# Low halves of the feed-forward projection's weight tiles from an accumulating transfer

## The chip, the cores and the metric

One core of a Trainium2 chip runs the whole program. The metric is the time of one execution on the device in microseconds, as the median of several runs; the profile is of one execution, taken by the hardware profiler.

## The reference

The program is one layer of a hybrid network on a sequence of 512 tokens of width 1024 in 32-bit floats: modulation of a normalised input, a mixer (an mLSTM beside an S5 state-space branch), a normalisation, a second modulation, and a gated feed-forward part. The change touches the first product of the feed-forward part alone:

```
def _conv_glu_ffn(h, w_ffn_up, w_ffn_conv, b_ffn_conv, w_ffn_down):
    val, gate = jnp.split(h @ w_ffn_up, 2, axis=-1)
    gate = jax.nn.gelu(_causal_dwconv(gate, w_ffn_conv, b_ffn_conv))
    return (gate * val) @ w_ffn_down
```

Here h is 512 x 1024 and w_ffn_up is 1024 x 5632, that is two halves of 2816 columns, or 2 x 22 tiles of 128 columns.

## The kernel before

The kernel gives TensorE its operands as float32r, and keeps the precision by splitting each operand into a high half (the operand written as float32r) and a low half (operand minus high half). A product is then the sum of three: high by high, high by low, low by high (`mm3`, L241 to L244). For a weight tile of 128 x 1024, `wsplit` (L224) does this in three steps: SP's queue loads the tile from HBM into a buffer w (`wload`, L215), ACT copies it into wh (L221), and DVE subtracts wh from w into wl (L210). There are 2 buffers of w, 3 of wh and 3 of wl; the next use of a buffer waits for the last reader of the one before.

The feed-forward projection has 44 such tiles, `h["wup"][u]`. Four of them (1, 0, 3, 2) are early: three use the three wh and wl buffers, one uses two others, and their products are taken over two halves of the tokens, each as soon as the normalised input of that half is there. The other 40 are split and multiplied in the loop over j (22 steps): first tile 2j + 1, the gate half, then tile 2j, the value half. A tile takes 8 times `mm3`, that is 24 matmuls of 512 columns, into a PSUM bank (`acc` for gate halves, 2 banks, and `hd` for value halves, 4 banks). The gate half goes through `gate_half`: POOL clears two columns of a buffer (L1183), ACT copies the bank behind them (L1184) and applies a scale and a bias (L1186), DVE adds the two other taps of the convolution (L202), and ACT and DVE compute the gelu (`gelu2`, L562 and L564). `val_half` multiplies by the value half (L207) and splits the result for the last product.

In the loop's steps 8 to 15, `ada2_step` also loads two 256 KB pieces of a modulation weight into buffers hh and adds them up on DVE.

The code is in program order, but the order of the instructions on each engine comes from a planner, which simulates the program with costs of its own and hands out each engine's instructions as they become ready there, those earlier in the program first; semaphores keep the dependencies. Each engine then runs its own queue in order, and transfers go out in the order of the queue that issues them. POOL issues no transfer in the kernel before; all go out on SP's queue.

Of the kernel before, what the change touches and what calls it, by code (L numbers as in the profile page):

```python
# [10 lines left out]
F32R = mybir.dt.float32r  # L11
I32 = mybir.dt.int32
AF = mybir.ActivationFunctionType
ALU = mybir.AluOpType
# [139 lines left out]
def build(tc, nc, h):  # L154
    with ExitStack() as ctx:
        _build(ctx, tc, nc, h)


def _build(ctx, tc, nc, h):
    V, A, T, GP = nc.vector, nc.scalar, nc.tensor, nc.gpsimd  # L160
# [4 lines left out]
    def tl(tag, shape, dt=F32, bufs=None, pool=None):  # L165
        uid[0] += 1
        return (pool or sb).tile(list(shape), dt, tag=tag, name=f"{tag}_{uid[0]}", bufs=bufs or BUFS[tag])
# [5 lines left out]
    def bank(tag):  # L173
        return tl(tag, [P, 512], pool=ps)
# [4 lines left out]
    def big(shape=(P, D), dt=F32, tag="hb"):  # L179
        return tl(tag, shape, dt)  # L180
# [10 lines left out]
    def dma(o, i):  # L191
        return nc.sync.dma_start(o, i)  # L192
# [16 lines left out]
    def sub(o, a, b):  # L209
        V.tensor_tensor(o, a, b, op=ALU.subtract)  # L210

    def f32(ap):
        return ap.bitcast(F32)

    def wload(ap, n=D, tag="w"):  # L215
        w = big(tag=tag)
        dma(w[:, :n], ap)
        return w

    def split_into(hi, lo, x):  # L220
        A.copy(hi, x)  # L221
        sub(lo, x, f32(hi))

    def wsplit(ap, n=D, tags=("wh", "wl"), w=None):  # L224
        w = wload(ap, n) if w is None else w
        wh, wl = (big(dt=F32R, tag=t) for t in tags)
        split_into(wh[:, :n], wl[:, :n], w[:, :n])
        return wh, wl

    def new_pair(tag):  # L230
# [494 lines left out]
    def kstep(j):  # L725
        wc = nxt[1]
        if j < KD - 1:
            nxt[:] = wa_load(j + 1), w0_load(j + 1)
        w0h, w0l = wsplit(None, NXM0 * P, w=wc)
        if j < KD - 1:  # L730
            pend = ada1_mm(j + 1, nxt[0])
        for m in range(NXM0):
            if j < KD - 1 and m == M1:
                ada1_cols(j + 1, *pend)
            if j < KD - 1 and m == M2:
                htr(j + 1)
            sl = slice(m * P, (m + 1) * P)
            mm3(acc0[m], w0h[:, sl], w0l[:, sl], hp[j][0], hp[j][1], j == 0, j == KD - 1)
# [13 lines left out]
    def ahead():  # L752
        while todo and len(ready) <= PF:
            ready.append(wsplit(todo.pop(0)))
        return ready.pop(0)
# [159 lines left out]
    def ada2_step(n=1):  # L915
        for _ in range(n):
            if not steps:
                return
            q, kc = steps.pop(0)
            if kc == 0:  # L920
                acc2[q] = [s5h(), s5h()]
            for i, a in enumerate(acc2[q]):
                wi = hh()
                dma(wi, h["wa2"][kc, :, q * D + i * 512:q * D + (i + 1) * 512])
                if kc == 0:
                    ts(a, wi, ca[:, 0:1])
                else:
                    stt(a, wi, ca[:, kc:kc + 1], a)
# [12 lines left out]
    def grow(i, factor):  # L941
        g = row(i)
        for n in range(2):
            o = bank("s5")
            for e, x in enumerate(pair_of(acc2[2 + i][n], "hh")):
                T.matmul(o, lhsT=onesr, rhs=x, start=e == 0, stop=e == 1)
            stt(g[n], o, 1.0, g[n], ALU.add, ALU.add)
            ts(g[n], g[n], factor)
        return g
# [45 lines left out]
    def scaled(src, g, st, tags=("wh", "wl")):  # L995
        w = wload(src)
        wh, wl = (big(dt=F32R, tag=t) for t in tags)
        for n in range(2):
            sl = slice(n * 512, (n + 1) * 512)
            x = w[:, sl] if st is None else tl(st, [P, 516])[:, :512]  # L1000
            tt(x, w[:, sl], g[n])
            split_into(wh[:, sl], wl[:, sl], x)
        return wh, wl
# [170 lines left out]
    def up_mm(o, w, c_):  # L1174
        for k in range(KD):
            sl = slice(k * P, (k + 1) * P)
            mm3(o[:, c_], w[0][:, sl], w[1][:, sl], h2[k][0][:, c_], h2[k][1][:, c_], k == 0, k == KD - 1)
# [3 lines left out]
    def gate_half(j, og):  # L1181
        gb_ = hh(514)
        GP.memset(gb_[:, 0:2], 0.0)  # L1183
        A.copy(gb_[:, 2:514], og)  # L1184
        a = hh()
        A.activation(a, og, AF.Identity, bias=col("fb", j), scale=col("fw", 44 + j))  # L1186
        for q in range(2):
            stt(a, gb_[:, q:q + 512], col("fw", 22 * q + j), a)
        gg = hh()
        gelu2(gg, a, hh)  # L1190
        return gg

    def val_half(j, gg, ov):
        tt(gg, ov, gg)
        gp_.append(pair_of(gg, "hp" if j < 8 else "hb" if j < 13 else "s5b" if j < 15 else "hx" if j < 18 else "gab"))

    early = [(u, wsplit(h["wup"][u], tags=("wh", "wl") if i < 3 else ("hb", "hb")), bank("hd"))
             for i, u in enumerate((1, 0, 3, 2)[:NS])]
    for hv in range(2):
# [10 lines left out]
    for j in range(NF):  # L1210
        if j == G2J:
            g2 = grow(1, 0.5)
        if j >= FJ:
            first.append(scaled(h["wfd"][len(first)], g2, None))
        ou = {}
        for u in (2 * j + 1, 2 * j):
            if u in pre:
                ou[u] = pre[u]
            else:
                w = wsplit(h["wup"][u])  # L1220
                ou[u] = bank("acc" if u % 2 else "hd")
                up_mm(ou[u], w, slice(0, 512))
            if u % 2:
                gg = gate_half(j, ou[u])
        val_half(j, gg, ou[2 * j])
        if 8 <= j < 16:
            ada2_step(1)
# [29 lines left out]
```

## Time and profile before

| what | value |
|---|---|
| median of 3 runs | 861.69 us (860.07 to 862.01) |
| span of the profiled execution | 862.0 us |
| TensorE busy | 828.5 us, 96% of the span |
| DVE busy | 607.1 us, 70% |
| ACT busy | 368.6 us, 43% |
| POOL busy | 98.0 us, 11% |
| read from HBM | 101.01 MB |

The span runs from the first to the last instruction of the profiled execution; no time around it is listed for that execution, so its own time is taken to be its span. The loop over the 40 tiles lies between about 506 and 730 us of it. In the rows, a line number such as L221 is that of the helper that issues the instruction, `wh<-w` names the tile that is written and those that are read, a bracket at the end of a row of the timeline is the idle time of the engine before that instruction and what ended it, and PE, DVE, ACT, POOL and SP are TensorE, VectorE, ScalarE, GpSimd and SyncE.

### The profile page before, as it was taken

How to read it: one execution, taken by the hardware profiler on the slowest of the kernel's cores; microseconds unless marked ns; L12 is line 12 of the kernel's file. 1: busy time of each engine (PE TensorE's matmuls, PEld its weight loads, DVE VectorE, ACT ScalarE, POOL GpSimd, SP SyncE). 2: the span in 40 equal slices, each digit the busy share in tenths (PEclk: the TensorE clock that was granted, in tenths of full speed). 3: DMA queues.
4: the chain of work that ended last, by engine and by line, in shares of the span. 5: the costliest groups of instructions: out<-in, count | busy, mean ns of one | idle time of the engine just before them, and what ended most of it. 6: DMA issues, size and time to landing. Idle time of an engine off the chain costs nothing.

```text
span 862.0 us, 11353 instructions
## 1 busy us (share of the span) xinstructions
PE 828.5 (96%) x4106; PEld 669.2 (78%) x4106; DVE 607.1 (70%) x1144; ACT 368.6 (43%) x589; POOL 98.0 (11%) x255
## 2 busy tenths in 40 slices
PE   3999999999999999999999999999999999999996
PEld 1777868778777778888887988888888878888785
DVE  5557978788689774578978767556777675878144
ACT  4454573564556442232334555444444444333000
POOL 2781211122022100000002200000000000000000
PEclk9999999999999999999999999999999999999998
DMA  9832132122222233568655023224444232445011
GB/s 336 288 132 86 53 101 62 45 85 62 79 60 87 86 123 122 196 203 294 210 191 177 2 74 102 94 98 147 146 147 137 86 120 74 171 163 169 11 49 49
DMA packets 45415, 105.94 MB, mean 123 GB/s; under 512 B 13360, under 2 KB 14256, under 8 KB 45360
## 3 DMA queue, kind: packets, MB, share of 16 engines
q1 hardware_dynamic: 45360, 105.23, 36.0%
q8 instruction: 32, 0.52, 0.2%
q14 instruction: 23, 0.19, 0.1%
HBM read 101.01 MB, written 2.10 MB: 120 GB/s over the span
## 4 chain that ended last, share of the span: by engine, by line
PE 76%; DVE 11%; ACT 4%; DMA 4%; issue 2%; SPq 2%; POOL 0%; DVEq 0%; ACTq 0%; POOLq 0%
PE acc L242 11%; PE acc L243 11%; PE acc L244 11%; PE hd L242 11%; PE hd L243 11%; PE hd L244 11%; DVE hh L202 2%; SPq L192 2%; DVE s5h L207 1%; PE s L242 1%; PE s L244 1%; PE s L243 1%; DVE wl L210 1%; PE s L612 1%; DMA w<-in_wmix 1%
## 5 line engine op out<-in xcount | busy, mean ns | idle before, releaser
L221 ACT CAST wh<-w 128x1024 fp32r<-128x1024 f32 (+2 forms) x103 | 103.2, 1003 | 144.0 <-PE acc L243 111.5
L210 DVE TENSOR_TENSOR wl<-w,wh 128x1024 fp32r<-128x1024 f32 (+2 forms) x103 | 120.5, 1172 | 60.8 <-ACT wh L221 60.1
L242 PE MATMUL acc<-hp,wh 128*128 128x512 f32 x256 | 103.4, 405 | 0.5 <-ACT hx L785 0.5
L244 PE MATMUL acc<-hp,wl 128*128 128x512 f32 x256 | 102.1, 399 | 0.0
L243 PE MATMUL acc<-hp,wh 128*128 128x512 f32 x256 | 102.1, 399 | 0.0
L242 PE MATMUL hd<-s5b,wh 128*128 128x512 f32 (+1 forms) x168 | 63.4, 380 | 0.7 <-ACT s5b L1169 0.5
L243 PE MATMUL hd<-s5b,wh 128*128 128x512 f32 (+1 forms) x168 | 63.6, 379 | 0.2 <-DVE s5b L210 0.2
L244 PE MATMUL hd<-s5b,wl 128*128 128x512 f32 (+1 forms) x168 | 63.3, 378 | 0.0
L242 PEld LDWEIGHTS acc<-hp,wh 128*128 128x128 f32 x256 | 48.2, 189 | 14.7 <-issue 3.7
L202 DVE SCALAR_TENSOR_TENSOR hh<-hh,hh 128x512 f32<-128x512 f32 x52 | 35.9, 691 | 31.2 <-ACT hh L564 14.7
L244 PEld LDWEIGHTS acc<-hp,wl 128*128 128x128 f32 x256 | 48.4, 189 | 11.2 <-issue 0.4
L243 PEld LDWEIGHTS acc<-hp,wh 128*128 128x128 f32 x256 | 48.4, 189 | 10.8 <-issue 0.4
L202 DVE SCALAR_TENSOR_TENSOR s5h<-hh,k,s5h 128x512 f32<-128x512 f32 x56 | 39.3, 746 | 4.7 <-DMA hh<-in_wa 4.6
L242 PEld LDWEIGHTS hd<-s5b,wh 128*128 128x128 f32 x168 | 31.3, 188 | 7.6 <-ACT s5b L1169 0.8
L243 PEld LDWEIGHTS hd<-s5b,wh 128*128 128x128 f32 x168 | 31.7, 189 | 7.0 <-DVE s5b L210 0.6
L244 PEld LDWEIGHTS hd<-s5b,wl 128*128 128x128 f32 x168 | 31.6, 188 | 6.4
L202 DVE SCALAR_TENSOR_TENSOR hh<-hh,k,hh 128x512 f32<-128x512 f32 x44 | 33.0, 751 | 4.5 <-ACT hh L1186 3.6
L1024 POOL TENSOR_SCALAR mov<-mov 128x1 f32<-128x1 f32 x6 | 3.7, 624 | 276.2 <-ACT s L1023 159.6
L244 PE MATMUL acc<-hx,wl 128*128 128x512 f32 x84 | 33.1, 394 | 0.0
L242 PE MATMUL acc<-hx,wh 128*128 128x512 f32 x84 | 33.1, 394 | 0.0
L243 PE MATMUL acc<-hx,wh 128*128 128x512 f32 x84 | 33.1, 394 | 0.0
L244 PE MATMUL acc<-s5b,wl 128*128 128x512 f32 x80 | 31.6, 395 | 0.5 <-DVE wl L210 0.5
(547 smaller groups left out, 2053.1 us busy)
## 6 DMA issues: line engine op xcount, KB each, us to landing
w<-in_wup SPq DMA_DIRECT2D x44, 512.0 KB, 3.2
hh<-in_wa SPq DMA_DIRECT2D x64, 256.0 KB, 4.2
w<-in_win SPq DMA_DIRECT2D x30, 512.0 KB, 3.2
w<-in_wfd SPq DMA_DIRECT2D x22, 512.0 KB, 3.3
hb<-in_wa SPq DMA_DIRECT2D x16, 512.0 KB, 7.4
w<-in_wglu SPq DMA_DIRECT2D x8, 512.0 KB, 3.3
w<-in_wdn SPq DMA_DIRECT2D x8, 512.0 KB, 3.3
w<-in_wmix SPq DMA_DIRECT2D x8, 512.0 KB, 4.2
```

The source lines that it names most:

```text
L192: return nc.sync.dma_start(o, i)
L202: V.scalar_tensor_tensor(o, i0, s, i1, op0=op0, op1=op1)
L207: V.tensor_tensor(o, a, b, op=op)
L210: V.tensor_tensor(o, a, b, op=ALU.subtract)
L221: A.copy(hi, x)
L242: T.matmul(o, lhsT=wh, rhs=xh, start=first, stop=False)
L243: T.matmul(o, lhsT=wh, rhs=xl, start=False, stop=False)
L244: T.matmul(o, lhsT=wl, rhs=xh, start=False, stop=last)
L612: T.matmul(o, lhsT=F[:, ri, pr, :], rhs=XB[:, ri, pr].rearrange("p g k -> p (g k)"), start=ri == 0, stop=False)
L1024: GP.tensor_scalar(v[:, 2:3], v[:, 0:1], v[:, 1:2], EPS * D, op0=ALU.add, op1=ALU.add)
```

## The change

The 40 tiles of the loop are split by a new function. The load of w and ACT's copy into wh stay. In place of DVE's subtraction, ACT writes the negated wh into wl, and then a transfer issued by POOL reads the same weight tile from HBM a second time and adds it to what stands in wl. The result is again the tile minus wh. DVE has no part in it. The four early tiles, and all other weights, are split as before by `wsplit`, which is unchanged.

```diff
--- before.py
+++ after.py
@@ -225,6 +225,14 @@
         w = wload(ap, n) if w is None else w
         wh, wl = (big(dt=F32R, tag=t) for t in tags)
         split_into(wh[:, :n], wl[:, :n], w[:, :n])
+        return wh, wl
+
+    def wsplit_dma(ap):
+        w = wload(ap)
+        wh, wl = (big(dt=F32R, tag=t) for t in ("wh", "wl"))
+        A.copy(wh, w)
+        A.activation(wl, f32(wh), AF.Copy, scale=-1.0)
+        GP.dma_start(wl, ap, accum_op=ALU.add)
         return wh, wl
 
     def new_pair(tag):
@@ -1217,7 +1225,7 @@
             if u in pre:
                 ou[u] = pre[u]
             else:
-                w = wsplit(h["wup"][u])
+                w = wsplit_dma(h["wup"][u])
                 ou[u] = bank("acc" if u % 2 else "hd")
                 up_mm(ou[u], w, slice(0, 512))
             if u % 2:
```

## Rows read from the trace of the kernel before

**Rows 1.** page: span, TensorE's busy time, transfers in 40 slices
```profile
span 862.0 us, 11353 instructions
...
PE 828.5 (96%) x4106; PEld 669.2 (78%) x4106; DVE 607.1 (70%) x1144; ACT 368.6 (43%) x589; POOL 98.0 (11%) x255
...
GB/s 336 288 132 86 53 101 62 45 85 62 79 60 87 86 123 122 196 203 294 210 191 177 2 74 102 94 98 147 146 147 137 86 120 74 171 163 169 11 49 49
```

**Rows 2.** one stretch: PE, PEld, DVE, ACT, POOL busy, clock, DMA share, GB/s
```profile
520.00:560.00 40.00, 40.00 (x174) 32.44 (x173) 26.65 (x34) 20.05 (x29) 0.40 (x4) 1.00 0.27 92
```

**Rows 3.** who TensorE waited for, 440 to 735 us
```profile
PE s L1163 <- ACT hx L1149: 0.9, 1, 0.9
...
PE acc L244 <- DVE wl L210: 0.5, 1, 0.5
```

**Rows 4.** timeline of ACT, start of the loop (start us, us, what)
```profile
505.14 1.05 ACT L221 CAST wh<-w 128x1024 fp32r<-128x1024 f32 x1 [6.31 <-PE hd L243]
506.09 0.58 ACT L1184 COPY hh<-hd 128x512 f32<-128x512 f32 x1
...
507.25 1.05 ACT L221 CAST wh<-w 128x1024 fp32r<-128x1024 f32 x1
```

**Rows 5.** timeline of DVE at the start of the loop
```profile
506.22 1.23 DVE L210 TENSOR_TENSOR wl<-w,wh 128x1024 fp32r<-128x1024 f32 x1 [6.91 <-ACT wh L221]
```

**Rows 6.** timeline of TensorE at the start of the loop
```profile
507.50 0.50 PE L244 MATMUL acc<-s5b,wl 128*128 128x512 f32 x1 [0.52 <-DVE wl L210]
```

**Rows 7.** timeline of all engines in the steady loop
```profile
568.17 0.40 PE L244 MATMUL acc<-hx,wl 128*128 128x512 f32 x1
...
568.40 0.39 PE L242 MATMUL hd<-s5b,wh 128*128 128x512 f32 x1
...
568.41 1.05 ACT L221 CAST wh<-w 128x1024 fp32r<-128x1024 f32 x1 [2.95 <-PE acc L243]
...
569.84 0.79 ACT L1186 ACTIVATE hh<-acc,k 128x512 f32<-128x512 f32 x1
...
573.97 0.39 PE L242 MATMUL acc<-s5b,wh 128*128 128x512 f32 x1
...
574.32 1.03 ACT L221 CAST wh<-w 128x1024 fp32r<-128x1024 f32 x1
```

**Rows 8.** groups of ACT by form, 505 to 735 us
```profile
L221 ACT CAST wh<-w 128x1024 fp32r<-128x1024 f32 x40 | 41.7, 1042 | 56.6 <-PE acc L243 44.8 <-PE hd L243 7.6 <-issue 4.2
```

**Rows 9.** groups of DVE by form, 505 to 735 us
```profile
L210 DVE TENSOR_TENSOR wl<-w,wh 128x1024 fp32r<-128x1024 f32 x40 | 48.8, 1220 | 43.5 <-ACT wh L221 43.5
```

**Rows 10.** who SP's queue waited for, 505 to 735 us
```profile
SPq L192 <- DVE wl L210: 225.5, 41, 36.0
```

**Rows 11.** page: transfers by tile, count, KB, us to landing
```profile
w<-in_wup SPq DMA_DIRECT2D x44, 512.0 KB, 3.2
...
hb<-in_wa SPq DMA_DIRECT2D x16, 512.0 KB, 7.4
```

**Rows 12.** groups of POOL by line, whole span
```profile
L786 POOL TENSOR_SCALAR hx<-hx,k 128x512 f32<-128x512 f32 x8 | 9.8, 1228 | 40.2 <-ACT hx L785 40.1
```

**Rows 13.** stretches at the end (columns as in Rows 2)
```profile
853.50:854.00 0.50, 0.33 (x3) 0.12 (x1) 0.14 (x1) 0.00 (x0) 0.00 (x0) 1.00 0.00 0
...
855.50:856.00 0.50, 0.00 (x0) 0.00 (x0) 0.43 (x3) 0.00 (x0) 0.28 (x2) 0.80 0.00 0
856.00:856.50 0.50, 0.00 (x0) 0.00 (x0) 0.50 (x2) 0.00 (x0) 0.50 (x1) 0.50 0.00 0
```

**Rows 14.** timeline of TensorE near the start of the span
```profile
21.83 0.63 PE L243 MATMUL acc<-hp,wh 128*128 128x512 f32 x1
22.25 0.63 PE L244 MATMUL acc<-hp,wl 128*128 128x512 f32 x1
```

**Rows 15.** timeline of POOL in the loop
```profile
589.66 0.10 POOL L1183 MEMSET hh<- 128x2 f32 x1 [11.77 <-DVE s5h L196]
```

**Rows 16.** transfers, 586 to 675 us: packets, MB, share
```profile
q1 hardware_dynamic: 4357, 12.12, 39.9%
```

## The prediction

> **What bounds the kernel now.** I read the page's busy shares first. TensorE is busy 828.5 of 862.0 us [rows 1]; that total hides which wait matters, so the second view is the table by stretch. Inside the feed-forward loop TensorE is busy 40.00 of 40 us while DVE has 26.65, ACT 20.05 and the transfers a share of 0.27 [rows 2]. So whatever only relieves DVE there can give nothing back. The third view, who TensorE waited for between 440 and 735 us, says the same from the other side: the longest wait is 0.9 us and the only one that touches a weight tile of this loop is a single 0.5 us wait for wl [rows 3].
>
> That wait is the key, and the timeline shows where it lies. The four early tiles hold all three wh and wl buffers until the last early matmuls. So the first tile of the loop cannot be split ahead: its cast starts at 505.14, the gate's copy (and its activation behind it) follows on ACT at 506.09, and the cast of the second tile comes at 507.25 [rows 4]. DVE writes wl from 506.22 for 1.23 us [rows 5], and TensorE, after the two products that need wh alone, goes on at 507.50, having waited 0.52 us [rows 6]. It is the one place where the making of wl sets TensorE's time.
>
> In the steady loop the making of wl has slack, and the reader should see how much. A tile is 24 matmuls; one starts every 0.23 us (568.17, 568.40), and tile boundaries lie at 568.40 and 573.97, 5.57 us apart [rows 7]. The cast at 568.41 fills a buffer released by the tile that has just ended, the third buffer back, so it is for the tile that starts 2 x 5.57 later, at 579.54, and wl is first read by that tile's third matmul, at 580.0. From the start of the cast that leaves 11.6 us [rows 7].
>
> **What the change removes.** 40 subtractions on DVE of 1,220 ns, 48.8 us [rows 9]. Taken at nothing: TensorE is the bound, and in the loop it waits for DVE nowhere but in the 0.5 us above [rows 2, 3]. The load of w goes out earlier, since its buffer is now released by the cast and not by DVE's subtraction, for which SP's queue waits 225.5 us in 41 waits [rows 10]; those loads already land in 3.2 us [rows 11] and nothing waits for them in the loop, so nothing either. The transfers of the modulation weights behind them on SP move up with them.
>
> **What it adds to ACT.** 40 negations. None stands in the trace; the nearest row is the cast of the same shape, 1,042 ns [rows 8], so 41.7 us, or 7.5 us in 40 where ACT has some 20 us free [rows 2]. They lengthen the way to wl, not TensorE's own work. Their place on ACT has two answers: right behind the cast, or behind the gate's copy and activation, as the second cast was at 507.25 although the buffers were free by then [rows 4]. I take the second; the first is 1.1 us earlier.
>
> **What it adds to POOL and to the transfers.** 40 accumulating transfers of 512 KB, read from HBM a second time. The trace holds no accumulating transfer and none issued by POOL, so the time from the negation's end to landing is bounded. Low: 3.2 us, what SP's load of the same 512 KB takes from issue to landing [rows 11]. High: two passes, each as slow as the slowest transfers of that size (7.4 us, when the queue was full) [rows 11], and 1.2 us on POOL, its longest kind of instruction [rows 12]: 16.0 us. I take 5.8: the 3.2, then 1.6 because the old content has to be fetched too (524,288 bytes at the 336 GB/s of the first slice [rows 1]), and 1.0 for POOL, inside its rows. It lies nearer the low end because the loop's transfers are one to three at a time, not the full queue of the start.
>
> The Trainium skill, "Collectives: The Full Stack", section "The bandwidth ceiling: the fold count and why AG ≠ RS ≠ AR", says that an add in a DMA engine costs nothing itself but makes it read two sources, so that such a transfer moves at half the rate of a copy; no run here shows it yet. By that rule the added 1.6 us stands; by SP's row alone it falls away and the sum below is 1.6 us less. The skill's page "DMA: Bandwidth & Descriptors", section "Anatomy of one DMA — SWDGE (gpsimd) path", puts a plain transfer from GpSimd at 2.0 us plus bytes over 436 GB/s, an estimate of 3.2 us for ours with POOL's part inside; by it the sum would be 1.0 us less.
>
> On POOL's queue the new issue stands between the gate's memsets of 0.10 us. The one at 589.66 runs when its buffer is freed [rows 15]; a transfer queued behind such a memset could go out some 2 us late, inside the slack below. A memset behind a transfer waits for the negation and about 1 us more; ACT's copy waits for it, and no TensorE wait hangs on that copy now.
>
> **The sum.** At the start of the loop: negation 507.25 to 508.30 (the place where the second cast stood [rows 4], 1.05 us), 5.8 us to landing, 514.1, TensorE goes on 0.05 us later as it does now [rows 5, 6]: 514.15 in place of 507.50, or 6.6 us lost. TensorE then comes out of an idle stretch of over 6 us. At the end of the span its last matmuls lie between 853.5 and 854.0, and the granted clock is 0.80 in the stretch from 855.5 and 0.50, 1.2 GHz, from 856.0 [rows 13]; so 2 us of idleness were enough there. What a matmul costs at the low clock is seen at the start: 512 columns go out 0.42 us apart (21.83, 22.25) [rows 14] against 0.23 in the loop [rows 7]. How long the low clock lasts is not shown for such a case. Between nothing and the whole first tile (24 x 0.19 = 4.6 us) I take half, 2.3 us.
>
> In the steady loop: from the cast at 568.41 the gate's activation ends at 570.63, the negation at 571.6, landing at 577.4, against 580.0 where it is needed [rows 7]: 2.6 us in hand, so TensorE waits for nothing. Where the cast comes behind the gelu (574.32, boundary at 573.97 [rows 7]) the negation can follow at once, ending at 576.3, and landing is allowed until 585.6: 9.2 us, 3.4 in hand. So the transfer may take up to 8.4 us in the one case and 9.2 in the other before TensorE waits. Second and third tile: the second negation ends by about 510.5 and lands by 516.5, while the first tile runs to 519 or later; the third follows 3 to 4 us on and has one tile more. Total 6.6 + 2.3 = 8.9 us. The profiled execution has a span of 862.0 us, nothing beyond it is shown, and it is 0.3 us over the median of 861.69: 870.9 for it, 870.6 for the median.
>
> **Rivals.** First: the transfer is slower than the slack, and the three wl buffers pace the loop. For it: the upper bound of 16.0. Against it: 512 KB land in 3.2 us. Price at 10 us: the start loses 10.8 + 2.3; then each chain of three tiles is short by 1.6 or 0.8, 1.2 on average, and there are (40 - 3) / 3 = 12.3 such steps, 15 us: 890. At 12 us it is 916, at 16.0 some 970. It decides from 8.4 us on.
>
> Second: transfers are crowded only where the modulation weights are also loaded. From 586 to 675 us the queue moves 12.12 MB in 89 us at a share of 39.9% [rows 16]. 1 MB more of read and fetch for each 5.57 us is 188 GB/s beside 136, so if both cost alike the share goes to 0.95 there, and landing could stretch to 10 us on some 16 tiles: 5.3 steps of 1.2, 6 us, 877 in all. Against it: elsewhere the share is 0.27 [rows 2] and stays near 0.8.
>
> Third, on the other side, not slower: TensorE fills the wait at the start with products that need wh alone. Two tiles have 32 of them, 7.4 us, so up to a landing at 514.5 nothing would be lost and the old wait of 0.5 goes: 861.2. It needs the order within one accumulating bank to be given up, or at least the next tiles' products to be put forward. Against it: at 507.50 TensorE waited 0.52 us for wl [rows 6] with the next product's wh ready.
>
> **Chances.** Loss at the start alone: 0.56. Slow transfer: 0.27. Crowding: 0.10. Filled wait: 0.07. The first gives the predicted time; its own range runs from 864.5 (negation right behind the cast, 3.2 us, full clock: +2.8) to 874. The range over the cases reaches to 900, a transfer of about 10.8 us; left out are the filled wait and slower transfers, about 0.18. About 0.2% (1.7 us) is what a measurement of this kernel can tell from no change. Filled wait splits into 0.05 within it and 0.02 faster; the rest, 0.93, is slower, since even the low bound costs 2.8 us.
>
> **What would show it.** Right: one TensorE wait of 5 to 8 us for the transfer near 507, a lower granted clock behind it, and a busy TensorE from there to 735. POOL issues 40 transfers landing in 4 to 8 us; DVE is 49 us less busy, ACT 42 more. Wrong: TensorE waits recurring each tile, landing above 8.4 us, POOL taking several us for one issue, or products on wh running ahead at the start.

## The result, and the profile after

The changed kernel takes 874.41 us (median of 4 runs, 873.61 to 874.94) against 861.70 for the kernel before on the same chip (4 runs, 860.07 to 862.01): a ratio of 1.015, 95% interval 1.0136 to 1.0164, 12.7 us slower. Forecast were 870.6 us and 864.5 to 900.

The page after: span, busy times, and what the transfers moved in 40 slices; then the two rows of weight transfers (median us from issue to landing).

```profile
span 872.1 us, 11442 instructions
...
PE 827.9 (95%) x4106; PEld 668.9 (77%) x4106; DVE 562.6 (65%) x1104; ACT 406.4 (47%) x629; POOL 133.5 (15%) x295
...
w<-in_wup SPq DMA_DIRECT2D x44, 512.0 KB, 3.5
wl<-in_wup POOLq DMA_DIRECT2D x40, 512.0 KB, 6.3
```

DVE is 44.5 us less busy than in [rows 1] and ACT 37.8 us more (forecast were 49 and 42). TensorE's busy time hardly moves, so the loss is looked for in its waits first; a busy total also hides matmuls that run at a lower clock, which come further down. Who TensorE waited for between 500 and 745 us (us in all, times, longest):

```profile
PE acc L252 <- DMA wl<-in_wup: 8.1, 2, 6.2
PE hd L250 <- ACT wh L233: 2.3, 1, 2.3
PE hd L252 <- DMA wl<-in_wup: 0.9, 1, 0.9
```

Before, [rows 3] had one wait of 0.5 us here. The new waits lie in two places, and neither is the steady loop. The first is the start of the loop; its timeline over all engines:

```profile
501.15 1.05 ACT L233 CAST wh<-w 128x1024 fp32r<-128x1024 f32 x1 [6.31 <-PE hd L251]
502.10 0.58 ACT L1192 COPY hh<-hd 128x512 f32<-128x512 f32 x1
502.22 6.30 SPq L192 DMA_DIRECT2D w<-in_wup  x3
...
503.25 1.05 ACT L234 ACTIVATE wl<-wh 128x1024 fp32r<-128x1024 f32 x1
...
504.63 1.11 POOL L235 DMA_DIRECT2D wl<-in_wup  x1 [13.89 <-ACT wl L234]
...
505.29 0.50 PE L250 MATMUL hd<-s5b,wh 128*128 128x512 f32 x1 [2.31 <-ACT wh L233]
505.63 0.40 PE L251 MATMUL hd<-s5b,wh 128*128 128x512 f32 x1
...
512.17 0.80 PE L252 MATMUL acc<-s5b,wl 128*128 128x512 f32 x1 [6.15 <-DMA wl<-in_wup]
512.77 0.63 PE L250 MATMUL acc<-s5b,wh 128*128 128x512 f32 x1
513.20 0.63 PE L251 MATMUL acc<-s5b,wh 128*128 128x512 f32 x1
```

The chain to read is cast 501.15, gate's copy 502.10, negation 503.25 to 504.30, transfer issued 504.63, landed 7.5 us later, just ahead of the matmul of 512.17. From the end of the negation to the landing that is 7.8 us. In between TensorE did two products of the second tile (505.29 and 505.63) and nothing else. Behind the wait the matmuls follow 0.43 us apart (512.77, 513.20) where the loop has 0.23 [rows 7]. The table by stretch shows why (columns as in [rows 2]):

```profile
506.00:508.00 2.00, 0.02 (x1) 0.00 (x0) 1.19 (x2) 2.00 (x3) 0.97 (x2) 0.96 0.91 172
508.00:510.00 2.00, 0.00 (x0) 0.00 (x0) 1.25 (x2) 2.00 (x5) 0.00 (x0) 0.50 1.05 207
...
516.00:518.00 2.00, 2.00 (x6) 1.52 (x6) 0.00 (x0) 0.00 (x0) 0.00 (x0) 0.50 0.90 178
518.00:520.00 2.00, 2.00 (x10) 1.66 (x9) 0.00 (x0) 0.00 (x0) 0.00 (x0) 0.98 0.05 8
...
520.00:560.00 40.00, 40.00 (x174) 32.41 (x174) 17.80 (x26) 27.14 (x37) 6.45 (x11) 1.00 0.79 178
```

The granted clock is 0.50, 1.2 GHz, from 508 to about 518 us: 14 matmuls each cost 0.2 us more, 2.8 us in all. The DMA share beside it is about 1, and the traffic by queue shows what the first transfer waited for. From 505 to 508.5 us POOL's queue (q0) moves nothing, and all that moves is on SP's (q1; packets, MB, share of the 16 engines):

```profile
q1 hardware_dynamic: 111, 0.45, 69.5%
```

It is the second of three loads of w (SP's row at 502.22), issued at 505.26, 0.6 us behind the transfer and moved ahead of it. From there on the transfer takes 3.6 us. The accumulating transfers of the second and third tile took 8.9 and 7.4 us from issue to landing, and the third load (508.19) 7.9 where the first took 3.1. From 518 on the last row holds: TensorE is busy 40.00 of 40 us, as in [rows 2], with DVE at 17.80 in place of 26.65.

The second place is the end of the loop, tiles 43 and 42. ACT and POOL there, and TensorE's wait:

```profile
716.03 1.12 ACT L221 CAST wh<-w 128x512 fp32r<-128x512 f32 x2
...
721.35 1.05 ACT L233 CAST wh<-w 128x1024 fp32r<-128x1024 f32 x1 [2.64 <-PE acc L251]
...
723.45 1.06 ACT L234 ACTIVATE wl<-wh 128x1024 fp32r<-128x1024 f32 x1
...
724.81 0.86 POOL L235 DMA_DIRECT2D wl<-in_wup  x1 [10.18 <-ACT wl L234]
...
730.18 0.50 PE L252 MATMUL acc<-s5b,wl 128*128 128x512 f32 x1 [1.91 <-DMA wl<-in_wup]
```

At 716.03 the first weight of the next projection (`scaled` in the last step of the loop) is cast into one of the three wh buffers. Two remain for the two tiles still to come, so the cast of tile 43 starts at 721.35, only 6.9 us ahead of the matmul that wants its wl (due at 728.27, 730.18 less the wait of 1.91). In the steady loop the distance is 11.3 to 11.6 us.

Matmul by matmul against the trace of before, the start costs 10.9 us and the end 3.4, together 14.3; between them the distance between the two traces doesn't change. The profiled execution of after reached the loop 4.0 us sooner than that of before (first cast 501.15 against 505.14 [rows 4]), though the order of instructions up to there is the same: 14.3 - 4.0 is, within 0.2, the difference of the spans, 10.1 us. The 4.0 us belong to the two executions and not to the change: 2.0 of them are there by 23 us, where the execution before kept its matmuls 0.42 us apart for longer [rows 14], and 1.5 more arise between 163 and 166 us, where its granted clock is 0.50, in this row of before, and that of after 1.00:

```profile
163.00:166.00 3.00, 3.00 (x16) 3.00 (x16) 2.98 (x4) 0.00 (x0) 0.00 (x0) 0.50 0.06 12
```

Two experiments below, unchanged up to the loop, make their first cast at 502.9. The execution after also lists a time of 873.92, 1.8 us beyond its span. The medians differ by 12.7 us and not by 14.3; where the other 1.6 us are isn't shown.

### The profile page after: what moved, and what is told of

Its sections match the earlier page's. It is cut to its first block, busy times and chain, and to the rows that moved or that the text cites. A ratio compares the mean times of both kernels' runs of the same rounds, so it can differ in the third digit from the quotient of the medians.

```text
span 872.1 us, 11442 instructions
## 1 busy us (share of the span) xinstructions
PE 827.9 (95%) x4106; PEld 668.9 (77%) x4106; DVE 562.6 (65%) x1104; ACT 406.4 (47%) x629; POOL 133.5 (15%) x295
## 4 chain that ended last, share of the span: by engine, by line
PE 75%; DVE 11%; ACT 5%; DMA 4%; issue 2%; SPq 2%; POOL 1%; DVEq 0%; ACTq 0%; POOLq 0%
PE hd L250 11%; PE acc L250 11%; PE acc L252 11%; PE acc L251 11%; PE hd L252 11%; PE hd L251 11%; DVE hh L202 2%; DMA wl<-in_wup 2%; SPq L192 2%; DVE s5h L207 1%; PE s L250 1%; PE s L251 1%; PE s L252 1%; PE s L620 1%; DVE wl L210 1%
## 5 line engine op out<-in xcount | busy, mean ns | idle before, releaser
L221 ACT CAST wh<-w 128x1024 fp32r<-128x1024 f32 (+2 forms) x63 | 61.5, 979 | 89.8 <-PE acc L251 68.4
L210 DVE TENSOR_TENSOR wl<-w,wh 128x1024 fp32r<-128x1024 f32 (+2 forms) x63 | 71.9, 1145 | 18.5 <-ACT wh L221 17.8
L233 ACT CAST wh<-w 128x1024 fp32r<-128x1024 f32 x40 | 41.7, 1042 | 61.5 <-PE acc L251 54.2
L235 POOL DMA_DIRECT2D wl<-in_wup x40 | 34.7, 868 | 202.7 <-ACT wl L234 202.7
L250 PEld LDWEIGHTS acc<-hp,wh 128*128 128x128 f32 x256 | 48.1, 188 | 14.3 <-issue 3.3
L251 PEld LDWEIGHTS acc<-hp,wh 128*128 128x128 f32 x256 | 48.2, 188 | 10.6 <-issue 0.4
L234 ACT ACTIVATE wl<-wh 128x1024 fp32r<-128x1024 f32 x40 | 42.3, 1058 | 0.5
```

Of the source, the lines that this page charges most:

```text
L233: A.copy(wh, w)
L234: A.activation(wl, f32(wh), AF.Copy, scale=-1.0)
L235: GP.dma_start(wl, ap, accum_op=ALU.add)
L250: T.matmul(o, lhsT=wh, rhs=xh, start=first, stop=False)
L251: T.matmul(o, lhsT=wh, rhs=xl, start=False, stop=False)
```

## The experiments

Each edit is to the changed kernel. Each ratio is to the kernel before, run on the same chip.

**The first two tiles by DVE.** Is the loss that of the tiles without a lead, or does every tile cost something?

```diff
-                w = wsplit_dma(h["wup"][u])
+                w = (wsplit if j == 2 else wsplit_dma)(h["wup"][u])
```

> The first two tiles of the loop (step 2) are split by DVE as before, the other 38 by the transfer. Theory (the loss is waits at places where the split has no lead, the rest of the loop is free): the wait of 6.2 us for the first tile and the low clock behind it (2.8 us) go, but the third tile, whose buffer of w comes free at 507.4 in the kernel before and whose cast stood at 511.3, now lands near 521 against 517.9 where it is needed: a new wait of about 3 us at the third tile, and 3.4 us stay at the last two. About 867 to 868 us. Rival (the second stream and POOL's queue slow every tile a little, and the waits only show it): 2 of 40 tiles give 0.6 us, 873.8. Second rival (one cold first transfer): the wait moves whole to the third tile, 872 or more.

Measured: 870.82 us, ratio 1.0112 (1.0097 to 1.0127). The time fell by less than the theory had, and the trace shows where the rest went:

```profile
PE acc L252 <- DMA wl<-in_wup: 5.7, 2, 3.9
```

The third tile became the first to be transferred, and TensorE waited 3.9 us for it (until 521.3), again with a granted clock of 0.50 behind it (522 to 524). Its transfer ran in the same crowd of w loads, at a share of 1.04 to 1.06. So the loss moved on by one pair of tiles and shrank; it did not move whole, as the second rival had it.

**The first four by DVE.** The same with `j in (2, 3)`.

> The first four tiles of the loop (steps 2 and 3) are split by DVE, the other 36 by the transfer. Theory: from the fifth tile on each split has three buffers' lead (11.6 us against some 10 needed), so the whole loss at the start goes, 10.9 us of waits and low clock by the two profiles; 3.4 us at the last two tiles stay: 863.5 (from the changed kernel) to 865 (from the kernel before). Rival (a cost in every tile): 4 of 40 give 1.3 us, 873.1. Rival (a cold first transfer): the wait comes back at the fifth tile.

Measured: 864.7 us, ratio 1.0037 (1.0024 to 1.005), as expected. The first accumulating transfer here (issued 520.81, with nothing else moving until 522.5) lands in 5.6 us, so the 7.5 us of the changed kernel is not what a first transfer costs: the cold-transfer rival is out. All that is left of the transfer's waits is the end of the loop:

```profile
PE acc L252 <- DMA wl<-in_wup: 1.9, 1, 1.9
PE hd L252 <- DMA wl<-in_wup: 1.0, 1, 1.0
```

**The last two by DVE.** With `j == NF - 1`.

> Only the last two tiles (step 21) are split by DVE, the other 38 by the transfer. Theory: in step 21 the first weight of the last product takes one of the three wh and wl buffers, so the last two tiles have the lead of two buffers (about 6 us) and not of three; DVE's subtraction fits into that, so the two waits near 730 and 737 us (1.9 and 0.9 us, 3.4 us with what stands beside them) go: 871.0 us. Rival (a cost in every tile): 2 of 40 give 0.6 us, 873.8.

Measured: 872.71 us, ratio 1.0128 (1.0112 to 1.0143). The waits of the end are gone, those of the start stay:

```profile
PE acc L252 <- DMA wl<-in_wup: 6.1, 1, 6.1
PE hd L250 <- ACT wh L233: 2.3, 1, 2.3
```

By the medians it saves 1.7 us, half of the 3.4 that the trace gives to the end. Against the next kernel, which has neither loss, the two sizes come out nearer the trace: the end alone costs 2.9 us (864.7 to 861.8), the start alone 10.9 (872.71 to 861.8).

**The first four and the last two by DVE.** With `j in (2, 3, NF - 1)`; 34 tiles still go by the transfer.

> The first four and the last two tiles are split by DVE, 34 by the transfer. Theory: nothing is lost in the middle, so the time is that of the kernel before, 861.7 us within 1.5, although 34 transfers, 18 MB of traffic and 34 negations on ACT remain. Rival (a cost in every tile): 34 of 40 stay, about 872.5 us.

Measured: 861.8 us (11 runs), ratio 1.0002 (0.999 to 1.0015). The whole loss is gone with six tiles, so 34 tiles by transfer cost nothing and give nothing. A cost in every tile is ruled out: 34 of 40 would have kept 85% of it. TensorE's only wait for a weight tile is the old one for DVE:

```profile
PE acc L252 <- DVE wl L210: 0.5, 1, 0.5
```

**A plain copy in place of the accumulation.** What does the adding itself cost? wl then holds the whole weight tile: this kernel leaves the subtraction out, and only its time is read.

```diff
-        GP.dma_start(wl, ap, accum_op=ALU.add)
+        GP.dma_start(wl, ap)
```

> The transfer on POOL is a plain copy from HBM into wl, without the addition onto the negated copy; everything else stands as in the changed kernel (wl then holds the whole weight tile, so the addition is the part left out). Theory (an accumulating transfer also fetches its destination, so it occupies the DMA engines about twice as long per byte): the share of the software queue about halves from 57% in 586 to 675 us, issue to landing falls from 5.4 to about 4 us in the quiet loop, the first wait falls by 1.5 to 2 us and the waits of the last two tiles by 1.4 each at most: about 870.5. Rival (what is slow is a transfer that POOL issues, whatever it does): landing and share stay, 874.4.

Measured: 870.27 us, ratio 1.0093 (1.0076 to 1.0111). The transfers of POOL's queue from 586 to 675 us, after and then in this kernel (packets, MB, share of the 16 engines):

```profile
q0 software_dynamic: 2304, 8.39, 57.2%
```

```profile
q0 software_dynamic: 2304, 8.39, 28.1%
```

The same 8.39 MB keep the engines twice as long (57.2 / 28.1 = 2.04) when they are added. The Trainium skill, "Collectives: The Full Stack", section "The bandwidth ceiling: the fold count and why AG ≠ RS ≠ AR", has an adding transfer read two sources and so move at half the rate; these two rows agree with it. From issue to landing the plain transfer takes 3.4 to 4.5 us in most of the quiet loop, the adding one 5.3 to 5.7. At the start the wait for wl is 3.4 us, not 6.15, and at the end there is none. The 2.3 us for the second tile's wh remain, and so does a low clock.

**Splitting the first pair ahead.** All 40 by transfer, but the first pair in two buffers of hb, which nothing holds until the last early matmuls.

```diff
-        wh, wl = (big(dt=F32R, tag=t) for t in ("wh", "wl"))
+        wh, wl = (big(dt=F32R, tag=t) for t in tags)
...
-                w = wsplit_dma(h["wup"][u])
+                w = wsplit_dma(h["wup"][u], ("hb", "hb") if j == 2 else ("wh", "wl"))
```

> All 40 tiles still go by negation and accumulating transfer, but the two tiles of the first step of the loop take two buffers of hb in place of wh and wl, so that nothing holds their buffers until the last early matmuls. Theory (the start loses because the first tile has no lead, not because a transfer is long): the first split moves ahead of the wait, the 6 us wait and the low clock behind it vanish, and the old 0.5 us wait too; the 3.4 us at the last two tiles stay: about 864.6. Rival (the first transfers are late because of what else the queues move there): a wait of several us stays, 870 or more.

Measured: 871.1 us, ratio 1.0104 (1.0086 to 1.0122). The place was right and the sum wrong. There is no wait for a transfer and no low clock at the start of the loop any more (from 505 to 525 us TensorE is busy 20.00 of 20), but the loss came back ahead of it. SP's queue, DVE and TensorE's wait:

```profile
465.90 13.73 SPq L192 DMA_DIRECT2D w<-in_wup  x2
479.73 1.08 SPq L192 DMA_DIRECT2D hx<-in_x  x2
```

```profile
486.55 0.69 DVE L202 SCALAR_TENSOR_TENSOR hx<-hx,acc 128x512 f32<-128x512 f32 x1 [3.41 <-DMA hx<-in_x]
```

```profile
PE s L1171 <- ACT hx L1157: 3.6, 1, 3.6
```

With the pair's splits moved ahead, their loads of w stand on SP's queue ahead of the last two loads of the residual input hx, and wait there for w buffers until 479.7; in the changed kernel all loads of hx are out by 467.4. They then share the engines with the early accumulating transfers, and the normalisation that waits for hx makes TensorE late: it is busy 5.05 of the 10 us from 490 to 500, and the granted clock averages 0.77 from 490 to 505. At the end of the loop one wait of 1.8 us stays.

**The negation on DVE.**

```diff
-        A.activation(wl, f32(wh), AF.Copy, scale=-1.0)
+        ts(wl, f32(wh), -1.0)
```

> The negation is done by DVE right behind the cast, not by ACT behind the gate's copy and activation. Theory: wl lands 1 to 1.5 us earlier at the start and at the last two tiles, so of the three waits there some 3 to 4 us go: 870.5 to 872. Rival (the transfer's own way, crowded with the loads of w, sets the landing): the first wait stays within 0.5 us, 874.

Measured: 873.05 us, ratio 1.0126 (1.0103 to 1.0148), below the changed kernel by the medians, with intervals that overlap; the 3 to 4 us of the theory did not come. The start, on DVE, POOL and TensorE:

```profile
504.01 0.69 DVE L196 TENSOR_SCALAR wl<-wh 128x1024 fp32r<-128x1024 f32 x1 [6.93 <-ACT wh L233]
505.03 1.11 POOL L235 DMA_DIRECT2D wl<-in_wup  x1 [12.54 <-DVE wl L196]
...
512.82 0.80 PE L252 MATMUL acc<-s5b,wl 128*128 128x512 f32 x1 [5.96 <-DMA wl<-in_wup]
```

From the cast (502.93 here) to the matmul it is 9.9 us, against 11.0 after (501.15 to 512.17). The chain is 1.1 us shorter, and the wait for the second tile's wh falls from 2.3 to 1.4. At the end nothing is gained: the last two transfers land in 6.2 and 6.3 us. The place of the negation is a small term, the transfer's own way the large one.

**Finding the break-even.** The prediction lets a transfer take 8.4 us (9.2 in the other case) before the steady loop waits. First a second, one-column transfer behind each:

```diff
         GP.dma_start(wl, ap, accum_op=ALU.add)
+        GP.dma_start(wl[:, 0:1], ap[:, 0:1], accum_op=ALU.add)
```

> Behind each accumulating transfer a second one adds the first column again (128 packets of 4 bytes), so the first column of wl is added twice. It tests the break-even of the steady loop, a transfer of 8.4 us from the end of the negation. Theory: the way to wl lengthens by 2 us or more; up to 8.4 us the loop stays free of waits and only the start and the last two tiles lose that much more (880 to 883); above it waits come back in every chain of three tiles, 1 us for each us above, 12 chains (890 or more). Rival (the loop is not sensitive to the transfer at all): 874.4 and no more than 2 us on top.

Measured: 910.82 us, ratio 1.0563 (1.0542 to 1.0583). This tested something else than meant. POOL, in the loop:

```profile
541.39 0.86 POOL L236 DMA_DIRECT2D wl<-in_wup  x1 [4.50 <-DMA wl<-in_wup]
541.93 1.22 POOL L235 DMA_DIRECT2D wl<-in_wup  x1
...
547.70 0.86 POOL L236 DMA_DIRECT2D wl<-in_wup  x1 [4.44 <-DMA wl<-in_wup]
```

The second transfer writes what the first has written, so POOL waits 4.4 us for the first to land, and all behind it on its queue waits too. One tile per 6.31 us (541.39 to 547.70) against the 5.57 that TensorE needs: POOL's queue paces the loop. It says nothing on the lead.

So the delay was put into POOL's own work, on the kernel with six tiles by DVE (861.8), where no wait stands in the way. POOL multiplies 512, 1,024 or 1,024 and then 512 columns of the negated copy by 1.0 ahead of its transfer:

```diff
+        GP.tensor_scalar(wl[:, :512], f32(wl)[:, :512], 1.0, None, op0=ALU.mult)
         GP.dma_start(wl, ap, accum_op=ALU.add)
```

> On the kernel that does the first four and the last two tiles by DVE (861.8, no wait for a transfer), POOL first multiplies 512 columns of the negated copy by 1.0 in place, then issues the transfer. The row of that shape before is 1.23 us, so the way from the end of the negation to landing goes from 5.5 to 6.7 us in the quiet loop and from at most 7.6 to 8.8 in the crowded steps. Theory (the steady loop waits only from 8.4 or 9.2 us on): at most 0.4 us on some chains, 862 to 863. Rival (each us of delay costs, tile by tile): a good part of 34 x 1.2 us, 870 or more.

> The same with all 1,024 columns, about 2.4 us: 7.9 us in the quiet loop, still free; up to 9.9 in the crowded steps, 1.5 and 0.7 us too late on some 5 chains of three tiles: about 868, and the waits of TensorE for wl lie between 590 and 690 us alone. Rival: waits everywhere in the loop, 885 or more.

> The same with 1,024 and then 512 columns, about 3.7 us: 9.2 us in the quiet loop, so 0.8 and 0.0 us too late on some 6 chains there; up to 11.2 in the crowded steps, 2.8 and 2.0 us on 5 chains: about 876, now with waits in the quiet stages too. Rival (the break-even is elsewhere): as e9b, waits in the crowded steps alone, or none.

Measured: 866.34 (1.0055, 1.0038 to 1.0073), 890.8 (1.0343, 1.0314 to 1.0373) and 919.11 us (1.0655, 1.06 to 1.0709). All three forecasts were too low, and the delays were larger than planned. In the first kernel the added row and, in the table by stretch, 530 to 590 and 590 to 690 us:

```profile
L235 POOL TENSOR_SCALAR wl<-wl 128x512 fp32r<-128x512 f32 x34 | 59.6, 1754 | 98.2 <-ACT wl L234 98.2
```

```profile
530.00:590.00 60.00, 60.00 (x260) 48.37 (x259) 24.01 (x35) 35.59 (x47) 28.29 (x28) 1.00 0.81 193
590.00:690.00 100.00, 99.06 (x427) 79.70 (x426) 47.70 (x67) 61.77 (x80) 48.47 (x44) 1.00 0.91 221
```

512 columns take 1.75 us, not 1.23, and 0.3 us pass from there to the issue: 2.05 us of delay on average. In the quiet stage the landing then comes 7.2 to 9.2 us after the end of the negation, and TensorE is busy 60.00 of 60. One wait of 0.9 us lies in the crowded steps, and one of 1.6 ends at 528.65, behind the first transfers. Where the break-even lies, two value halves of the crowded steps show, each with its negation on ACT and the matmul that wants wl:

```profile
659.72 1.06 ACT L234 ACTIVATE wl<-wh 128x1024 fp32r<-128x1024 f32 x1
...
669.48 0.47 PE L253 MATMUL hd<-s5b,wl 128*128 128x512 f32 x1
```

```profile
602.92 1.06 ACT L234 ACTIVATE wl<-wh 128x1024 fp32r<-128x1024 f32 x1
...
613.50 0.47 PE L253 MATMUL hd<-s5b,wl 128*128 128x512 f32 x1 [0.88 <-DMA wl<-in_wup]
```

The first landed at 669.34 (issued 663.12, 6.2 us), 8.6 us after its negation, and its matmul came about 0.2 us late; the second landed at 613.36 (606.33, 7.0 us), 9.4 us after it, and TensorE stood for 0.9 us. So a value half may take about 8.4 us. A gate half in the quiet stage took 9.2 us (negation to 552.97, landing 562.12) and delayed its matmul by about 0.1. These are the two figures of the prediction, 8.4 and 9.2, within 0.1 us. The profiled execution is the fastest of seven (864.20); why the median lies 2.1 us above it isn't shown.

With 1,024 columns the delay is 3.0 + 0.3 us, and the waits stand in the quiet stages too:

```profile
PE hd L253 <- DMA wl<-in_wup: 17.1, 8, 3.1
```

One of them ends at 552.6, in the quiet stage. Above the break-even the price was set too low: the prediction's own formula (1.2 us for each of 11 chains at 10 us) gives 14 us for this kernel, which is 29 above its base. In the trace 18.6 us are waits for wl (17.1 here, 1.5 at one gate half) and about 7 lie in some 40 matmuls behind them that ran slower (granted clock 0.50 from 552 to 558, and 0.57 on average from 630 to 634 and from 657 to 661); the rest isn't placed. The waits are longer than 1.2 us because these tiles take longer than 10: all eight of this row are value halves, and in the first seven, where the wait is 2.0 to 3.1 us, landing comes 10.6 to 11.7 us after the negation. Their transfers take 7.0 to 8.1 us where others take 5.2 to 5.8, and each is still under way when the next is issued; that this overlap is what slows them is likely, and not shown.

The third kernel says no more on the lead. From 530 to 690 us its POOL works 131.0 us on 23 tiles, 5.7 a tile, beside the 5.57 that TensorE needs, so POOL's own pace is in its time as well.

## Why the prediction was right, and where it was not

The sign and the place were right, and the measured 874.4 lies in the range. The sum was 4 us short: two mis-sized terms and one that is missing. By the traces they make 8.1 + 2.8 + 3.4 = 14.3 us, against 8.9 forecast and 12.7 by the medians. The low end of the forecast, +2.8 us, is 3.0 by its own terms (6.65 less 2.6 and 1.06).

- **DVE's subtractions at nothing**: right. 34 tiles without them give 861.8, ratio 1.0002.
- **ACT's negation hidden, behind the gate's copy and activation**: right; 501.15 to 503.25 is the forecast distance of 2.1 us ([rows 4]: 505.14 to 507.25).
- **5.8 us to landing**: right in the quiet loop (negation to 578.43, issue 578.71, landing 5.3 us later: 5.6), and so were its parts: 1.5 us or so for the adding, about 4 us for the plain transfer. Wrong at the start, 7.8. The step that failed is the one that had moved the w loads up, taken them at nothing because nothing waits for them, and priced the transfer as one of one to three that don't hinder each other. They don't hold TensorE by a wait of their own, but one of them moved ahead of the transfer that does: its first bytes moved 4.0 us after its issue, against 1.6 in the quiet loop (the transfer of 578.71) and 1.8 for the first transfer of the kernel with four tiles by DVE. No run takes that load away alone. The start wait became 8.1 us against 6.6: 2.0 more for the landing, less 0.5 for the two products put forward (two at 0.23).
- **Low clock, 2.3 us**: the trace shows 2.8. The prediction's reading that 2 us of idleness were enough at the end of the span does not carry over: here the clock is still 1.00 behind the waits of 2.3 us (at 505.29) and 1.9 us (at 730.18), and it falls at about 508.
- **The steady loop free**: right, and the margins, 8.4 and 9.2 us, are as worked out.
- **The end of the loop**: missing, 3.4 us in the trace. The lead of 11.6 us was worked out from three buffers and taken to hold for every tile after the start. In the last step another weight takes one of them. The subtraction hid this: cast and subtraction take about 2.3 us, far inside the 6.9 that remain.
- **Crowding as a rival**: the share in 586 to 675 us was forecast at 0.95 and is 0.98; landing rises to 7.7 us from the issue, 7.9 from the negation's end, under the 8.4. No wait follows, so the crowded steps cost nothing, with 0.5 us to spare.
- **Filled wait**: two products ran ahead, 0.5 of the 7.4 us that this rival needed.
- **Slow transfer**: not at 5.6 us; the delayed kernels show that it would have been the largest loss, with 1,024 columns at about twice the price given.

By the other page, "DMA: Bandwidth & Descriptors" of the Trainium skill, section "Anatomy of one DMA — SWDGE (gpsimd) path", a plain transfer was estimated at 3.2 us; the plain transfer here takes longer, 3.4 to 4.5 in most of the quiet loop.

## What to carry to other kernels

Taking work off an engine that isn't the bound gives nothing, and what replaces it is priced by its latency where the lead is shortest, not by its average: look for the first tile, the last tiles, and each place where another user takes a buffer of the same pool. A load that moves up "for nothing" may still lengthen a transfer that is on the path, and an operation that moves ahead takes its place on the queue with it, as the loads of hx showed. If such a transfer is wanted for its own sake, use it only for the tiles with a full lead: 34 of 40 here, at no cost.

## What had not been expected of the hardware

An accumulating transfer also holds POOL longer than a plain one. The groups of POOL in the changed kernel and, second, in the one with the plain copy (count, us in all, mean ns):

```profile
L235 POOL DMA_DIRECT2D wl<-in_wup x40 | 34.7, 868 | 202.7 <-ACT wl L234 202.7
L1191 POOL MEMSET hh<- 128x2 f32 x21 | 9.1, 435 | 0.0
```

```profile
L235 POOL DMA_DIRECT2D wl<-in_wup x40 | 21.4, 536 | 212.4 <-ACT wl L234 212.4
L1191 POOL MEMSET hh<- 128x2 f32 x21 | 2.5, 118 | 0.0
```

Issuing takes 0.87 us against 0.54, and the small memset 0.44 against 0.12 (0.10 before [rows 15]); in the timeline it stands right behind the issue. The same POOL multiplication of 512 columns took 1.75 us beside these transfers where a similar row before has 1.23 [rows 12]; the runs don't tell whether the transfers, the in-place operands or something else make the difference.
